# A planned decoder layer: buffers at the places that the plan gave them, from a first build that plans and a second that emits

## The chip, the cores and the metric

The kernel runs on one core of a Trainium2 chip. The metric is the device time of one execution in microseconds (us), as the median of several runs. One execution was also taken with the hardware profiler; its rows are what the prediction argues from.

## The reference

One hybrid decoder layer on 512 tokens of width 1024, all in float32:

```
h = rms_norm(x, mix_norm_g);  proj = h @ w_in           # 512 + 512 + 768 + 24 + 2048 columns
u, q, kv, nsa_g, merge_g = split(proj)
y_pool = pooling_mixer(u) @ w_pool_out                  # windows 2, 4, 8, 16; four 128-wide groups
y_nsa  = nsa_mixer(q, kv, sigmoid(nsa_g)) @ w_nsa_out   # 8 heads of 64, 2 kv groups, 3 branches:
                                                        #   compressed blocks, selected blocks, window
x = x + (gate_pool * y_pool + gate_nsa * y_nsa) @ w_out # gates: sigmoid of merge_g
h = rms_norm(x, ffn_norm_g)
gate_pre, val = split(h @ w_up)                         # 2 x 2816 columns
out = x + (silu(causal_dwconv(gate_pre)) * val) @ w_down
```

## The kernel before, in words

Activations lie transposed (features on the 128 partitions, 512 tokens along the row). Every float32 factor is split into a high part and a rest, both of a type that TensorE (PE) multiplies in one pass, so a product is three matmuls: high by high, high by rest, rest by high. A weight tile arrives in `wraw` by a transfer that SyncE (SP) issues; ScalarE (ACT) makes `whi`, and the rest `wlo` comes either from a subtraction on VectorE (DVE) or from an accumulating transfer that GpSimd (POOL) issues. In the attention part the q and k tiles (`qp`, `kp`) are normalised and rotated by DVE, transposed by PE against `ident` (in the constants `cs`) and copied and split into `qt` and `kt`. The second half of the layer, from the merge of the two mixers on, uses a seven-product scheme for most 2x2 blocks of weights (tiles `r1`, `r2`, `s3` and their parts `sh`, `sl`).

The stages lie in the profile about so: the first projections 0 to 60 us, attention with the remaining projections mixed in 60 to 260, the merge and output projection 260 to 345, the feed-forward part 345 to 640, the last down projection 640 to 675.

**What sets the order.** The layer is not emitted as it is written. The class `Plan` records every call as an `Op`, with dependences by tile region, and `emit` runs a small model of the engines (`run`, with costs from `price`) under many settings: which of two PE streams goes first, how late a transfer lands. A trial's order is run again, held fixed, under four settings of lateness and rate (`TRIALS`); the order with the smallest sum of modelled ends is emitted, call by call. All recorded calls are therefore issued from one line, and every row of the profile bears the line L431.

**What sets the places.** `Plan.tile` asks a pool for a tile under a tag with so many buffers: 60 pages `pg` of 128 x 512, rings of three for `wraw`, `whi` and `wlo`, ten `pp`, six `pt`, and in PSUM two banks `mm`, three `tr`, one `av` and `sc` with the rest. In the model, a new tile takes the place that came free first (`past = min(f)` in `run`, `free` keyed by tag). In the build, the framework's pool chooses among the places of the tag by itself. An instruction that first writes a tile waits for the users of the tile that had the place before.

Of the kernel before, what the change touches and what calls it, by code (L numbers as in the profile page):

```python
# [2 lines left out]

# [5 lines left out]
F32 = mybir.dt.float32  # L9
# [6 lines left out]
P = 128  # L16
T = 512
NT = 4
D = 1024
KD = 8  # L20
# [47 lines left out]
RATE = 331000.0  # L68
SHARE = 1.5
LANDS = (0.8, 0.8, 1.2, 1.2, 2.0, 2.0)  # L70
TRIALS = ((0.5, RATE), (0.8, RATE), (1.4, RATE), (0.8, 0.9 * RATE))
AHEAD = 4
RUN = 12

# [21 lines left out]
class Op:  # L96
# [3 lines left out]
    def __init__(self, i, eng, stream):  # L100
        self.i, self.eng, self.stream = i, eng, stream
        self.calls, self.cost, self.tail, self.land = [], 0.0, 0.0, 0
        self.deps, self.succ, self.allocs, self.tiles = set(), [], [], set()
        self.due, self.port = 0.0, False
# [9 lines left out]
        return call  # L114


class Plan:
    OUT = ("out", "accum_out", "ap")
    FIFO = ("wraw", "whi", "wlo")

    def __init__(self, nc):
# [81 lines left out]
    def price(self, eng, method, outs, ins, a, kw):  # L203
        n = max(_cols(x) for x in outs + ins)
        if method == "dma_start":
            x = outs[0]
            size = x.ap[0][1] * _cols(x) * 4 if hasattr(x, "ap") else 0
            return (0.87 if eng == "POOL" else 0.45), 0.0, size * (2.0 if kw.get("accum_op") is not None else 1.0)
        if eng == "PE":
            n = _cols(a[2])  # L210
            return max(n / 2250.0 + (0.005 if n < 300 else 0.0), 0.109), 0.17, 0
        if eng == "ACT":
            c = 0.19 + n * 0.000835
            if any(_cols(x) == 1 for x in ins):
                c += 0.09
            if kw.get("accum_out") is not None:
                c += 0.19
            if a[2] in (AF.Sin,):
                c += 1.28
            return c, 0.0, 0  # L220
        if eng == "DVE":
            wide = [x for x in ins if _cols(x) > 1]
            if method == "tensor_tensor_reduce":
                return 0.24 + n * 0.00105, 0.0, 0
            if len(wide) > 1 or method == "tensor_reduce" or any(x.tensor.name in self.psum for x in wide):
                return 0.15 + n * (0.00105 if method != "scalar_tensor_tensor" else 0.00114), 0.0, 0
# [5 lines left out]
    def run(self, key, reserve, land, rate=RATE, fixed=None):  # L232
        ops = self.ops
        ahead = 0 if fixed else AHEAD
        engs = ("PE", "ACT", "DVE", "POOL", "SP")
        free = {t: [(0.0, "")] * c for t, c in self.caps.items()}
# [19 lines left out]
        def finish(o):  # L256
            for n in o.tiles:
                left[n] -= 1
                if not left[n]:
                    free[self.tag[n]].append((max(u.fin for u in self.users[n]) + 0.06, n))  # L260
            for s in o.succ:
                s.left -= 1
                s.ready = max(s.ready, o.start + o.cost if s.eng == o.eng and not o.land else o.fin + 0.06)
                if not s.left and s.eng != "PE":
                    pool[s.eng].append(s)

        def settle(limit):
            while True:
                act = [(1.0 if e == "POOL" else SHARE, l) for e, l in queue.items() if l and l[0][0] <= now[0]]
                both = sum(q for q, _ in act)  # L270
                t = min((l[0][0] for l in queue.values() if l and l[0][0] > now[0]), default=1e18)
                head = None
                if act:
                    q, l = min(act, key=lambda x: x[1][0][1] / x[0])
                    if now[0] + l[0][1] / q * both <= t:
                        t, head = now[0] + l[0][1] / q * both, l
                if t > limit:
                    return False
                for q, l in act:
                    l[0][1] -= (t - now[0]) * q / both  # L280
                now[0] = t
                if head:
                    o = head.pop(0)[2]
                    o.fin = t + (self.lands[o.i] if land is None else land)
                    finish(o)
                    return True

        def when(o):
            t = o.ready
            for n in o.allocs:  # L290
                g = self.tag[n]
                f = free[g]
                if g in nxt and self.rank[n] != nxt[g] or n in self.early and self.early[n] != line[0]:
                    return None
                if len(f) <= (0 if g != "pg" else ahead if n in self.early else reserve if o.stream == "f" else 0):
                    return None
# [31 lines left out]
        while len(order) < len(ops):  # L328
            best = None
# [24 lines left out]
            for n in o.allocs:  # L354
                g = self.tag[n]
                f = free[g]
                past = min(f)
                f.remove(past)
                for u in self.users.get(past[1], ()):
# [8 lines left out]
        settle(1e17)  # L368
        while settle(1e17):
            pass  # L370
        return order, max(clock.values())

    def dues(self, order):
        lost, end, due = 0.0, 0.0, {}
# [11 lines left out]
    marks = ()  # L386

    def emit(self, tries, reserve):
        for n, u in self.users.items():
            for o in u:  # L390
                o.tiles.add(n)
        for o in self.ops:
            for d in o.deps:
                self.ops[d].succ.append(o)
        start = [float(o.i) for o in self.ops]
        part = [sum(m <= o.i for m in self.marks) for o in self.ops]
        parts = len(self.marks) + 1
# [2 lines left out]
        for cut in (0,) + CUTS:  # L400
            key, seen = start, []
            for i in range(tries + (MORE if cut else 0)):
# [4 lines left out]
                self.lands = [lands[p] for p in part]  # L407
                order, _ = self.run(key, reserve, None)
# [5 lines left out]
                for late, rate in TRIALS:  # L414
                    again, span = self.run(key, 0, late, rate, fixed)
                    spans += span
                    end = 0.0
                    for o in again:
                        if o.eng == "PE":
                            lost[part[o.i]] += max(0.0, o.start - end)  # L420
                            end = o.start + o.cost
                seen.append((lost, used, lands))
                if best is None or spans < best[0]:
                    best = (spans, order)
            last = seen[:tries]
            ahead = [c for c in CUTS if c > cut]
            if ahead:
                _, frozen, frozen_land = min(seen, key=lambda x: sum(x[0][:ahead[0]]))
        for o in best[1]:
            for method, a, kw in o.calls:  # L430
                getattr(self.real[o.eng], method)(*a, **kw)  # L431


@with_exitstack
def hybrid_layer(ctx: ExitStack, tc: tile.TileContext, xT, xa, pos, par, cst, poolw, w1, wa, wb, wf,
                 wpo, wno, wout, wup, wdn, wdz, out):
    nc = tc.nc
    pl = Plan(nc)
# [1193 lines left out]
```

## Time and profile before

| | before |
|---|---|
| median of 3 runs | 680.16 us (680.01 to 680.59) |
| the profiled execution's own time | 680.19 us |
| its span, first to last instruction | 678.1 us |
| PE busy (matmuls) | 673.4 us, 99% of the span |
| weight loads of PE (PEld) busy | 609.1 us, 90% |
| DVE busy | 545.2 us, 80% |
| ACT busy | 458.7 us, 68% |
| POOL busy | 109.0 us, 16% |
| mean rate of the transfers | 172 GB/s |

A matmul's row begins where it starts and ends where its last result is modelled to be written, so rows of neighbours overlap; how fast PE really works is read from the distance of starts, and a stretch without a row is an idle PE. "Idle before" names what ended a gap. SPq and POOLq rows are issues of transfers.

### The profile page before, as it was taken

How to read it: one execution, taken by the hardware profiler on the slowest of the kernel's cores; microseconds unless marked ns; L12 is line 12 of the kernel's file. 1: busy time of each engine (PE TensorE's matmuls, PEld its weight loads, DVE VectorE, ACT ScalarE, POOL GpSimd, SP SyncE). 2: the span in 40 equal slices, each digit the busy share in tenths (PEclk: the TensorE clock that was granted, in tenths of full speed). 3: DMA queues.
4: the chain of work that ended last, by engine and by line, in shares of the span. 5: the costliest groups of instructions: out<-in, count | busy, mean ns of one | idle time of the engine just before them, and what ended most of it. 6: DMA issues, size and time to landing. Idle time of an engine off the chain costs nothing.

```text
span 678.1 us, 11960 instructions
## 1 busy us (share of the span) xinstructions
PE 673.4 (99%) x4294; PEld 609.1 (90%) x4294; DVE 545.2 (80%) x1198; ACT 458.7 (68%) x857; POOL 109.0 (16%) x138
## 2 busy tenths in 40 slices
PE   9999999999999999999999999999999999999998
PEld 8898888888888888988889999999999999999997
DVE  6869678788887867788888998887778787899983
ACT  7666577776677765347788867677657677675741
POOL 0010111010110110001322312222213122220121
PEclk9999999999999999999999999999999999999999
DMA  8469646263565555846977958779858678553774
GB/s 306 145 156 264 172 108 187 67 171 99 143 167 134 143 134 181 312 146 203 232 166 176 194 144 203 194 170 208 190 160 190 168 161 211 134 115 129 191 181 109
DMA packets 51179, 116.41 MB, mean 172 GB/s; under 512 B 5808, under 2 KB 9264, under 8 KB 51120
## 3 DMA queue, kind: packets, MB, share of 16 engines
q1 hardware_dynamic: 32688, 76.44, 33.9%
q0 software_dynamic: 18288, 39.07, 32.6%
q8 instruction: 34, 0.56, 0.3%
q14 instruction: 25, 0.20, 0.1%
q10 hardware_dynamic: 144, 0.14, 0.1%
HBM read 70.28 MB, written 6.29 MB: 113 GB/s over the span
## 4 chain that ended last, share of the span: by engine, by line
PE 99%; DMA 1%; SPq 0%; ACT 0%; DVE 0%; issue 0%
PE mm L431 38%; PE tr L431 36%; PE sc L431 13%; PE av L431 12%; DMA wraw<-wa 1%; SPq L431 0%; ACT whi L431 0%; DVE o L431 0%
## 5 line engine op out<-in xcount | busy, mean ns | idle before, releaser
L431 ACT ACTIVATE whi<-wraw 128x1024 fp32r<-128x1024 f32 (+4 forms) x99 | 91.9, 930 | 40.9 <-PE sc L431 14.7
L431 DVE TENSOR_TENSOR wlo<-wraw,whi 128x1024 fp32r<-128x1024 f32 (+3 forms) x73 | 74.0, 1015 | 5.1 <-ACT whi L431 4.3
L431 PE MATMUL tr<-tl,sh 128*128 128x256 f32 x261 | 73.1, 280 | 0.0
L431 PE MATMUL mm<-xh,whi 128*128 128x512 f32 x176 | 70.7, 402 | 0.0
L431 PE MATMUL tr<-th,sh 128*128 128x256 f32 x250 | 70.4, 282 | 0.0
L431 PE MATMUL tr<-th,sl 128*128 128x256 f32 x250 | 70.4, 282 | 0.0
L431 PE MATMUL mm<-xh,wlo 128*128 128x512 f32 x176 | 68.9, 391 | 0.0
L431 PE MATMUL mm<-xl,whi 128*128 128x512 f32 x176 | 68.6, 390 | 0.0
L431 POOL DMA_DIRECT2D sl<-r x46 | 39.8, 866 | 149.8 <-ACT sl L431 104.8
L431 POOL DMA_DIRECT2D wlo<-wraw x26 | 22.3, 858 | 231.7 <-ACT wlo L431 178.8
L431 PEld LDWEIGHTS tr<-tl,sh 128*128 128x128 f32 x261 | 49.3, 189 | 0.2
L431 PEld LDWEIGHTS tr<-th,sh 128*128 128x128 f32 x250 | 47.0, 188 | 0.7
L431 PEld LDWEIGHTS tr<-th,sl 128*128 128x128 f32 x250 | 47.0, 188 | 0.0
L431 ACT ACTIVATE wlo<-wraw 128x1024 fp32r<-128x1024 f32 x26 | 27.6, 1060 | 19.3 <-PE mm L431 18.4
L431 PEld LDWEIGHTS mm<-xh,wlo 128*128 128x128 f32 x176 | 33.0, 188 | 7.3
L431 PEld LDWEIGHTS mm<-xl,whi 128*128 128x128 f32 x176 | 33.1, 188 | 6.2
L431 ACT ACTIVATE pp<-pp,asm 128x384 f32<-128x384 f32 (+3 forms) x64 | 35.4, 556 | 4.9 <-DVE asm L431 4.9
L431 PEld LDWEIGHTS mm<-xh,whi 128*128 128x128 f32 x176 | 33.1, 188 | 6.1
L431 DVE SCALAR_TENSOR_TENSOR ft<-fg,pr,ft 128x511 f32<-128x511 f32 (+1 forms) x44 | 32.9, 749 | 7.0 <-ACT ft L431 6.3
L431 POOL DMA_DIRECT2D sl<-wraw x26 | 22.4, 862 | 84.7 <-ACT sl L431 68.5
L431 ACT ACTIVATE sh<-wraw 128x512 fp32r<-128x512 f32 x52 | 32.3, 620 | 4.1 <-DVE wraw L431 4.0
L431 ACT ACTIVATE sl<-r 128x512 fp32r<-128x512 f32 x46 | 28.6, 622 | 9.3 <-DMA r<-wup 5.4
(443 smaller groups left out, 2134.4 us busy)
## 6 DMA issues: line engine op xcount, KB each, us to landing
wlo<-wraw POOLq DMA_DIRECT2D x26, 512.0 KB, 4.6
wraw<-wup SPq DMA_DIRECT2D x23, 512.0 KB, 4.1
sl<-r POOLq DMA_DIRECT2D x46, 256.0 KB, 4.8
wraw<-wf SPq DMA_DIRECT2D x22, 512.0 KB, 3.6
r<-wup SPq DMA_DIRECT2D x42, 256.0 KB, 5.7
sl<-wraw POOLq DMA_DIRECT2D x26, 256.0 KB, 4.2
wraw<-wdn SPq DMA_DIRECT2D x16, 320.0 KB, 3.7
sl<-s POOLq DMA_DIRECT2D x17, 256.0 KB, 5.0
```

Source lines behind the costliest of these rows:

```text
L431: getattr(self.real[o.eng], method)(*a, **kw)
```

## The change

Four things are altered, all in the planning code.

The kernel function is built twice. In the first build, `Plan` has no `made`; it plans, and instead of emitting it raises `Planned` with two lists, the order of the ops and for each tile the number of the place that the model gave it. The second build is given these lists: `tile` makes each place a pool entry of its own (tag and place number, one buffer), and `emit` writes the ops in the stored order.

In the model, `free` now holds for each place when it comes free, its number and its last tile; `run` notes in `taken` which place each tile took, and a run with a fixed order can also hold the places fixed (`slots`), so that a tile waits for its own place rather than for the first free one.

The trials by which an order is judged grow from four to seven: three with a lateness drawn at random for each op (0.5 to 1.8, for one op in 25 up to 3.0 more).

The price of a PE matmul changes: a float32 matmul that is not a transpose counts as two passes, and 0.005 is added below 500 columns rather than below 300.

```
+class Planned(Exception):
+    pass
...
     def tile(self, pool, shape, dt, name, tag, bufs, psum=False):
-        t = pool.tile(list(shape), dt, name=name, tag=tag, bufs=bufs)
+        if self.made:
+            slot = self.made[1][len(self.homes)]
+            t = pool.tile(list(shape), dt, name=name, tag="%s.%d" % (tag, slot), bufs=1)
+        else:
+            t = pool.tile(list(shape), dt, name=name, tag=tag, bufs=bufs)
         n = t.tensor.name
+        self.homes.append(n)
...
-            return max(n / 2250.0 + (0.005 if n < 300 else 0.0), 0.109), 0.17, 0
+            passes = 2 if method == "matmul" and a[1].dtype == F32 else 1
+            return passes * max(n / 2250.0 + (0.005 if n < 500 else 0.0), 0.109), 0.17, 0
...
-                t = max(t, min(f)[0])
+                if slots is None:
+                    t = max(t, min(f)[0])
+                else:
+                    at_slot = [x[0] for x in f if x[1] == slots[n]]
+                    if not at_slot:
+                        return None
+                    t = max(t, at_slot[0])
...
     def emit(self, tries, reserve):
+        if self.made:
+            for i in self.made[0]:
+                for method, a, kw in self.ops[i].calls:
+                    getattr(self.real[self.ops[i].eng], method)(*a, **kw)
+            return
...
+        trials = [([late] * len(self.ops), rate) for late, rate in TRIALS]
+        for seed in range(RANDOM):
+            r = random.Random(seed)
+            trials.append(([r.uniform(0.5, 1.8) + (r.random() < 0.04) * r.uniform(0.0, 3.0) for _ in every], RATE))
...
-        for o in best[1]:
-            for method, a, kw in o.calls:
-                getattr(self.real[o.eng], method)(*a, **kw)
+        raise Planned(best[1], [best[2].get(n, 0) for n in self.homes])
```

Both programs hold the same instructions, each with the same operands; what differs is their order on an engine, the places, and so the waits. POOL's order is the same row for row. PE's order is the same up to the transposes of q and k near 53 us and again from the end of attention on; between them blocks of 2 to 12 matmuls change places. ACT, DVE and SP differ in many places by a few rows. Three places follow; the change's rows bear L413, the line from which its second build issues.

**SP, the first loads.** `wraw` are weights of the first projection (`wa`), `xr` and `x0` parts of x. Before:

```order
L431 DMA wraw_82<-wa 128x512
L431 DMA x0_67<-xa 128x256
L431 DMA wraw_82<-wa 128x256
L431 DMA xr_87<-xT 128x512
L431 DMA wraw_91<-wa 128x768
L431 DMA xr_88<-xT 128x512
L431 DMA wraw_97<-wa 128x768
L431 DMA xr_94<-xT 128x512
```

Now:

```order
L413 DMA wraw_82<-wa 128x512
L413 DMA x0_67<-xa 128x256
L413 DMA wraw_82<-wa 128x256
L413 DMA wraw_91<-wa 128x768
L413 DMA xr_87<-xT 128x512
L413 DMA wraw_97<-wa 128x768
L413 DMA xr_88<-xT 128x512
L413 DMA xr_94<-xT 128x512
```

The weights of the second round (`wraw_91`) are issued ahead of x's second part (`xr_87`), and those of the third (`wraw_97`) ahead of `xr_88`.

**PE, the transposes of the first two k tiles**, `tr_193`, among the matmuls of the first gate projection, `mm_231`, near 59 us. Before:

```order
L431 MATMUL mm_231<-xh_113,whi_229 128x512
L431 MATMUL mm_231<-xl_114,whi_229 128x512
L431 MATMUL mm_231<-xh_113,wlo_230 128x512
L431 MATMUL mm_231<-xh_119,whi_229 128x512
L431 MATMUL mm_231<-xl_120,whi_229 128x512
L431 MATMUL mm_231<-xh_119,wlo_230 128x512
L431 MATMUL mm_231<-xh_133,whi_229 128x512
L431 MATMUL mm_231<-xl_134,whi_229 128x512
L431 MATMUL mm_231<-xh_133,wlo_230 128x512
L431 MATMUL tr_193<-cs_65,kp_151 128x128 x2
L431 MATMUL tr_193<-cs_65,kp_152 128x128 x2
L431 MATMUL tr_199<-cs_65,qp_149 128x128 x4
```

Now:

```order
L413 MATMUL tr_193<-cs_65,kp_151 128x128 x2
L413 MATMUL tr_193<-cs_65,kp_152 128x128 x2
L413 MATMUL mm_231<-xh_113,whi_229 128x512
L413 MATMUL mm_231<-xl_114,whi_229 128x512
L413 MATMUL mm_231<-xh_113,wlo_230 128x512
L413 MATMUL mm_231<-xh_119,whi_229 128x512
L413 MATMUL mm_231<-xl_120,whi_229 128x512
L413 MATMUL mm_231<-xh_119,wlo_230 128x512
L413 MATMUL mm_231<-xh_133,whi_229 128x512
L413 MATMUL mm_231<-xl_134,whi_229 128x512
L413 MATMUL mm_231<-xh_133,wlo_230 128x512
L413 MATMUL mm_236<-xh_85,whi_234 128x512
```

The four k transposes stand nine matmuls earlier, and the transposes of the third q tile (`tr_199`) no longer follow them.

**DVE, the rotation of those tiles** (`kp_151`, `kp_152` of k, `qp_149` of q; `rt` are products with the sine), near 54 to 58 us. Before:

```order
L431 SCALAR_TENSOR_TENSOR vv_182<-mm_181,rstd_70,vv_182 128x4x64
L431 TENSOR_TENSOR qp_149<-tr_77,small_81 128x512
L431 TENSOR_TENSOR qt_188<-tr_186,qt_188 64x512
L431 TENSOR_TENSOR kp_151<-kp_151,gkv_140 128x256
L431 TENSOR_TENSOR kp_152<-kp_152,gkv_140 128x256
L431 TENSOR_TENSOR rt_184<-kp_151,rope_138 128x64
L431 TENSOR_TENSOR rt_185<-kp_152,rope_138 128x64
L431 TENSOR_TENSOR rt_189<-qp_149,ropeq_143 128x128
L431 TENSOR_TENSOR kp_151<-kp_151,rope_138 128x4x16
L431 TENSOR_TENSOR kp_152<-kp_152,rope_138 128x4x16
L431 TENSOR_TENSOR qt_187<-tr_186,qt_187 64x512
L431 TENSOR_TENSOR kp_151<-kp_151,rt_184 128x4x16
```

Now:

```order
L413 TENSOR_TENSOR kp_151<-kp_151,gkv_140 128x256
L413 TENSOR_TENSOR kp_152<-kp_152,gkv_140 128x256
L413 TENSOR_TENSOR rt_184<-kp_151,rope_138 128x64
L413 TENSOR_TENSOR rt_185<-kp_152,rope_138 128x64
L413 TENSOR_TENSOR qp_149<-tr_77,small_81 128x512
L413 TENSOR_TENSOR kp_151<-kp_151,rope_138 128x4x16
L413 TENSOR_TENSOR kp_152<-kp_152,rope_138 128x4x16
L413 TENSOR_TENSOR kp_151<-kp_151,rt_184 128x4x16
L413 TENSOR_TENSOR kp_152<-kp_152,rt_185 128x4x16
L413 SCALAR_TENSOR_TENSOR vv_182<-mm_181,rstd_70,vv_182 128x4x64
L413 TENSOR_TENSOR qt_188<-tr_186,qt_188 64x512
L413 TENSOR_TENSOR rt_189<-qp_149,ropeq_143 128x128
```

The k tiles' last additions move ahead of `vv_182`, of the two splits of the first q tile (`qt_188`, `qt_187`, the latter now the next row) and of `rt_189`.

**ACT in a feed-forward step** near 387 us: `u1` and `tr` are copies out of and between PSUM banks, `whi_1036` the high part of a down projection's weights, `ft_985` the gate's silu, `sh` and `sl` parts of weight sums. Before:

```order
L431 ACTIVATE u1_982<-tr_980 128x256
L431 ACTIVATE whi_1036<-wraw_1035 128x640
L431 ACTIVATE ft_985<-ft_985 128x512
L431 ACTIVATE tr_1005<-mm_1004 128x256
L431 ACTIVATE sl_1019<-r2_1015 128x512
```

Now:

```order
L413 ACTIVATE u1_982<-tr_980 128x256
L413 ACTIVATE sh_1003<-wraw_988 128x512
L413 ACTIVATE tr_1005<-mm_1004 128x256
L413 ACTIVATE whi_1036<-wraw_1035 128x640
L413 ACTIVATE ft_985<-ft_985 128x512
```

The copy `tr_1005`, which the next products of PE accumulate onto, now stands ahead of `whi_1036` and `ft_985`.

More of the change, by code (lines that the diff above doesn't have):

```diff
@@ L1 @@
 import math
+import random
 from contextlib import ExitStack, contextmanager, nullcontext
@@ L71 @@
 TRIALS = ((0.5, RATE), (0.8, RATE), (1.4, RATE), (0.8, 0.9 * RATE))
+RANDOM = 3
 AHEAD = 4
@@ L119, with __init__ @@
     FIFO = ("wraw", "whi", "wlo")
-    def __init__(self, nc):
+    def __init__(self, nc, made):
+        self.made, self.homes = made, []
         self.real = {"PE": nc.tensor, "ACT": nc.scalar, "DVE": nc.vector, "POOL": nc.gpsimd, "SP": nc.sync}
@@ L230, in price, with run @@
         return 0.33 + n * 0.0025, 0.0, 0
-    def run(self, key, reserve, land, rate=RATE, fixed=None):
+    def run(self, key, reserve, lands, rate=RATE, fixed=None, slots=None):
         ops = self.ops
@@ L235, in run @@
         engs = ("PE", "ACT", "DVE", "POOL", "SP")
-        free = {t: [(0.0, "")] * c for t, c in self.caps.items()}
+        free = {t: [(0.0, i, "") for i in range(c)] for t, c in self.caps.items()}
+        taken = {}
         nxt = {t: 0 for t in self.FIFO}
@@ L259, in finish @@
                 if not left[n]:
-                    free[self.tag[n]].append((max(u.fin for u in self.users[n]) + 0.06, n))
+                    free[self.tag[n]].append((max(u.fin for u in self.users[n]) + 0.06, taken[n], n))
             for s in o.succ:
@@ L283, in settle @@
                     o = head.pop(0)[2]
-                    o.fin = t + (self.lands[o.i] if land is None else land)
+                    o.fin = t + lands[o.i]
                     finish(o)
@@ L356, in run @@
                 f = free[g]
-                past = min(f)
+                past = min(f) if slots is None else [x for x in f if x[1] == slots[n]][0]
                 f.remove(past)
-                for u in self.users.get(past[1], ()):
+                taken[n] = past[1]
+                for u in self.users.get(past[2], ()):
                     u.hand.append(o)
@@ L370, in run @@
             pass
-        return order, max(clock.values())
+        return order, max(clock.values()), taken
     def dues(self, order):
@@ L394, in emit @@
                 self.ops[d].succ.append(o)
+        every = range(len(self.ops))
+        trials = [([late] * len(self.ops), rate) for late, rate in TRIALS]
+        for seed in range(RANDOM):
+            r = random.Random(seed)
+            trials.append(([r.uniform(0.5, 1.8) + (r.random() < 0.04) * r.uniform(0.0, 3.0) for _ in every], RATE))
         start = [float(o.i) for o in self.ops]
@@ L406, in emit @@
                 lands = [frozen_land[p] if p < cut else LANDS[i % len(LANDS)] for p in range(parts)]
-                self.lands = [lands[p] for p in part]
-                order, _ = self.run(key, reserve, None)
+                order, _, slots = self.run(key, reserve, [lands[p] for p in part])
                 used = key
@@ L413, in emit @@
                 spans, lost = 0.0, [0.0] * parts
-                for late, rate in TRIALS:
-                    again, span = self.run(key, 0, late, rate, fixed)
+                for late, rate in trials:
+                    again, span, _ = self.run(key, 0, late, rate, fixed, slots)
                     spans += span
@@ L423, in emit @@
                 if best is None or spans < best[0]:
-                    best = (spans, order)
+                    best = (spans, [o.i for o in order], slots)
             last = seen[:tries]
@@ L428, in emit @@
                 _, frozen, frozen_land = min(seen, key=lambda x: sum(x[0][:ahead[0]]))
-        for o in best[1]:
-            for method, a, kw in o.calls:
-                getattr(self.real[o.eng], method)(*a, **kw)
+        raise Planned(best[1], [best[2].get(n, 0) for n in self.homes])
 @with_exitstack
 def hybrid_layer(ctx: ExitStack, tc: tile.TileContext, xT, xa, pos, par, cst, poolw, w1, wa, wb, wf,
-                 wpo, wno, wout, wup, wdn, wdz, out):
+                 wpo, wno, wout, wup, wdn, wdz, out, made=None):
     nc = tc.nc
-    pl = Plan(nc)
+    pl = Plan(nc, made)
     PE, ACT, DVE, POOL, SP = pl.engines
@@ L1622 @@
     arrays = _layout(**inputs)
-    nc = _bacc.Bacc("TRN2", target_bir_lowering=False, num_devices=1, dynamic_dma_scratch_size=4096)
-    args = [nc.dram_tensor(n, a.shape, _mybir.dt.from_np(a.dtype), kind="ExternalInput").ap()
-            for n, a in arrays.items()]
-    args.append(nc.dram_tensor("out", (KD, P, T), F32, kind="ExternalOutput").ap())
-    with _tile.TileContext(nc) as tc:
-        hybrid_layer(tc, *args)
+    made = None
+    for _ in range(2):
+        nc = _bacc.Bacc("TRN2", target_bir_lowering=False, num_devices=1, dynamic_dma_scratch_size=4096)
+        args = [nc.dram_tensor(n, a.shape, _mybir.dt.from_np(a.dtype), kind="ExternalInput").ap()
+                for n, a in arrays.items()]
+        args.append(nc.dram_tensor("out", (KD, P, T), F32, kind="ExternalOutput").ap())
+        try:
+            with _tile.TileContext(nc) as tc:
+                hybrid_layer(tc, *args, made=made)
+        except Planned as plan:
+            made = plan.args
     r = _run(nc, [arrays], core_ids=[0])
```

## The prediction

> **What bounds the kernel now.** I read the page's busy times first, then PE's waits, then the stretches, then the chain that ended last.
>
> ```profile
> span 678.1 us, 11960 instructions
> PE 673.4 (99%) x4294; PEld 609.1 (90%) x4294; DVE 545.2 (80%) x1198; ACT 458.7 (68%) x857; POOL 109.0 (16%) x138
> ...
> PE mm L431 <- POOL ones L431: 1.0, 1, 1.0
> PE sc L431 <- ACT whi L431: 0.3, 1, 0.3
> ```
>
> The two last rows are the whole list of PE's waits: 1.0 us before its very first matmul and 0.3 us once more, in 678.1 us. The next rows are stretches (us, then busy time of each engine with its number of instructions, then granted clock) and, last, their sum over six stretches from 6.45 to 674.76.
>
> ```profile
> 60.00:260.00 200.00, 200.00 (x1069) 169.00 (x1068) 157.79 (x477) 144.90 (x305) 21.25 (x29) 1.00 0.56 144
> 345.00:400.00 55.00, 55.00 (x445) 54.07 (x444) 50.01 (x93) 44.10 (x83) 12.18 (x15) 1.00 0.77 174
> sum 668.31, PE 668.31 PEld 604.59 DVE 543.25 ACT 455.93 POOL 108.55; mean PE 111.39 PEld 100.76 DVE 90.54 ACT 75.99 POOL 18.09
> ```
>
> From 6.45 us to 674.76 us, PE is busy for 668.31 of 668.31 us. Since a matmul's row lasts longer than the distance to the next start, a wait of some tenths could hide in that. So I look at distances, in the chain of waits (start, us, what) and in the group of one kind of matmul.
>
> ```profile
> 131.80 2.79 PE mm L431 x12
> 207.58 2.72 PE mm L431 x12
> 358.42 2.83 PE tr L431 x24
> 378.28 2.83 PE tr L431 x24
> 656.30 2.84 PE tr L431 x24
> ...
> L431 PE MATMUL mm<-xh,whi 128*128 128x512 f32 x176 | 70.7, 402 | 0.0
> ```
>
> Twelve 512-wide matmuls take 2.72 to 2.79 us, or 0.227 to 0.233 each; 24 of width 256 take 2.83 or 2.84, or 0.118 each, early in the feed-forward part and at its end alike. The stream is evenly packed: no stage has slower matmuls that better placement could speed up. The kernel is bound by the number of its matmuls, with a head before 6.45 and a tail behind 674.76:
>
> ```profile
> 1.64 4.31 DMA wraw<-wa
> 6.45 0.74 PE sc L431 x4
> ...
> 674.48 0.28 PE L431 MATMUL tr<-yth,sl 128*128 128x256 f32 x1
> 674.80 0.42 DVE L431 TENSOR_TENSOR o<-x,tr 128x256 f32<-128x256 f32 x1 [1.00 <-PE tr L431]
> ```
>
> The head is the first weights' landing at 5.95 (1.64 + 4.31) and a cast; the tail is one addition and a store, 678.1 - 674.76 = 3.3 us.
>
> **The change part by part.** The trials, the new price of a matmul and the two builds run on the host while the program is made; none is an instruction, so each costs nothing on the chip except through the order and the places they lead to. No matmul is added, removed or resized. PE's 668.31 us therefore stay, and the sum asks only what the new order and places add as waits.
>
> *What can be gained.* Of the waits, the 1.0 us ends with the constant that POOL writes and stays. The 0.3 us ends with the cast of the weights that land at 5.95; that transfer is SP's third issue before and now, so it stays too. Bound: 0 to 0.3 us.
>
> *SP's first loads.* The landings are read from what waited for them:
>
> ```profile
> 6.80 0.72 ACT L431 ACTIVATE xh<-xr,x 128x512 fp32r<-128x512 f32 x1 [0.40 <-DMA xr<-xT]
> 7.95 0.83 ACT L431 ACTIVATE whi<-wraw 128x768 fp32r<-128x768 f32 x1
> 9.83 0.87 PE L431 MATMUL tr<-whi,xh 128*128 128x512 f32 x3
> ```
>
> The part of x lands by 6.80 and the weights of round two by 7.95, so 1.15 us lie between them (an upper estimate, since ACT may have come later than the landing). Swapped, the weights land by about 5.95 + 1.15 = 7.10 and their cast ends at 7.93; x lands by 7.95 and its cast ends at 8.67. PE needs both at 9.83. Before, the later of the two ended at 7.95 + 0.83 = 8.78. The margin goes from 1.05 to about 1.16 us: cost nothing; PE's first round covers it, and without that cover a late cast would stand in full.
>
> *The k transposes near 59 us.* All rows of this step, DVE first:
>
> ```profile
> 53.72 0.47 DVE L431 SCALAR_TENSOR_TENSOR vv<-mm,rstd,vv 128x256 fp32r<-128x256 f32 x1
> 55.02 0.69 DVE L431 TENSOR_TENSOR qt<-tr,qt 64x512 fp32r<-64x512 f32 x1 [0.23 <-ACT qt L431]
> 56.70 0.28 DVE L431 TENSOR_TENSOR rt<-qp,ropeq 128x128 f32<-128x128 f32 x1
> 57.28 0.69 DVE L431 TENSOR_TENSOR qt<-tr,qt 64x512 fp32r<-64x512 f32 x1
> 58.00 0.36 DVE L431 TENSOR_TENSOR kp<-kp,rt 128x64 f32<-128x64 f32 x2
> 61.80 0.69 DVE L431 TENSOR_TENSOR kt<-tr,kt 64x512 fp32r<-64x512 f32 x1 [0.89 <-ACT kt L431]
> 62.52 0.69 DVE L431 TENSOR_TENSOR th<-mm,rb 128x512 f32<-128x512 f32 x1
> 63.77 0.29 DVE L431 TENSOR_TENSOR qp<-qp,rt 128x128 f32<-128x128 f32 x1
> ...
> 59.49 1.06 ACT L431 ACTIVATE wlo<-wraw 128x1024 fp32r<-128x1024 f32 x1 [3.41 <-PE mm L431]
> 59.29 0.60 PE L431 MATMUL tr<-cs,kp 128*128 128x128 f32 x4
> 64.25 0.60 PE L431 MATMUL tr<-cs,qp 128*128 128x128 f32 x4
> ```
>
> PE comes to the k transposes nine matmuls earlier: 9 x 0.228 = 2.05 us, at 57.24 instead of 59.29. On DVE the last additions move ahead of four instructions: 0.47 + 0.69 + 0.28 + 0.69 = 2.13 us. They ended at 58.36 and should end at 56.23. The first transposes had 59.29 - 58.2 (the first of the two additions) = about 1.1 us of margin and keep it: 2.13 gained against 2.05 spent. The next narrow place is the fourth q tile: its addition ends at 64.06 and PE starts at 64.25, a margin of 0.19. There PE comes three matmuls earlier, 0.68 us, and DVE's `th` of 0.69 moves behind the addition: the margin stays at 0.20. It even grows where ACT no longer puts its 1.06 us `wlo` ahead of the copy for which DVE stood 0.89 us. If that cover failed, each tenth late there would be a tenth of PE's time. I take nothing; bounds -0.1 and +0.9 us (DVE standing for ACT again, at the new place).
>
> *ACT in the feed-forward.*
>
> ```profile
> 387.10 0.73 ACT L431 ACTIVATE whi<-wraw 128x640 fp32r<-128x640 f32 x1
> 388.25 0.38 ACT L431 ACTIVATE tr<-mm 128x256 f32<-128x256 f32 x1
> 399.55 3.43 PE sc L431 x15
> ```
>
> The copy still cannot run before PE has its sum, at 388.25, so ACT now stands for it, and the weight cast behind it starts near 388.6 instead of 387.10: 1.5 us late. DVE's rest of those weights is late by as much, and so is SP's next load into that ring. The down projection that uses them starts at 399.55, 11 us after the cast. ACT is busy 44.10 of 55 us in this stretch, so it makes good the 1.5 us. Cost nothing; the cover is the distance of 11 us.
>
> *The places.* The trace shows no address and no cost of one. Bounds come from the twelves, which lie on different tiles: the 176 first matmuls of the quoted kind stand for 176 x 3 / 12 = 44 twelves; had all the shortest or the longest time instead of the middle, they would give 44 x 0.035 = 1.5 us either way. I take 0, since no stretch differs. As waits, places matter where a new tile must wait for the old one's users; PE's list shows no such wait before, so nothing is there to remove, and one that the plan adds counts as an order's delay.
>
> The sum: 678.1 + 0 + 0 + 0 = 678.1 of span; the profiled execution took 680.19, 2.1 more, and lies within 0.03 of the median 680.16. Forecast: **680.2 us**.
>
> **The rivals.** (a) *Slower: the supply at the start of the feed-forward.* In 345 to 400 us DVE is busy 50.01 of 55, and weight parts arrive just before use:
>
> ```profile
> L431 POOL DMA_DIRECT2D sl<-r x3: 860/862/862, 374.5 to 383.8; - x3
> DMA to landing us min/median/max: 3.4/7.1/7.8
> 382.60 0.28 PE L431 MATMUL tr<-th,sl 128*128 128x256 f32 x1
> ```
>
> A part issued at 374.5 that takes 7.8 us lands at 382.3, and PE reads such a part at 382.60: 0.3 us of margin. A feature repeats every (378.28 - 358.42) / 2 = 9.93 us, so this stretch holds five. If the swaps make these parts late by one DVE instruction of 0.69, PE waits 0.4 in each: 5 x 0.4 = 2.0 us, 682.2 us. It decides from the fourth feature on. For it: the thin margin, and ACT and DVE rows that trade places. Against it: PE's and POOL's orders are unchanged there, and the work ahead of these very parts on ACT is the same.
>
> (b) *Faster: hidden waits go.* The 44 twelves fall to 2.72 us each: 1.5 us less, 678.7. For it: the spread. Against it: a twelve's end is a neighbour's start, so the spread comes with the neighbour's kind.
>
> (c) *Faster: free time behind the weight loads.* Between 60 and 260 us, where most of PE's order changes, no weights are loaded for 200.00 - 169.00 = 31.0 us. If the new order filled a tenth of that, 3.1 us, the time would be 677.1. The Trainium skill, "Perfetto Trace Analysis", section "Identifying the Most-Contended Engine", says that matmul busy time is a poor measure of how near PE is to its limit, and that the busy share of weight loads is a good one. By that rule the 90% leave room. The trace speaks against it: with 0.228 us from start to start and a load per matmul, loads pause because 512 columns stream, not because something is late.
>
> (d) *The change does not do what it says:* the second build's places differ from the plan, or come to the same waits. Then the time is that of the order alone, 680.2 as well.
>
> **How the numbers follow.** The forecast has a chance of 0.74, (d) 0.03, (a) 0.17, (b) 0.04, (c) 0.02. A measurement of this kernel can tell about 0.2%, 1.36 us, from no change. So "same", 678.8 to 681.5, has 0.74 + 0.03 = 0.77; slower 0.17; faster 0.04 + 0.02 = 0.06. The forecast's own range is 679.6 (0.3 gained, and 0.3 for the runs) to 681.1 (the 0.9 at the k transposes). Widened above to (a) with 0.2 for the runs, and below by some more tenths towards (b), it is 679.3 to 682.4, which leaves out (b), (c) and a longer (a), about 0.1.
>
> **What would show it.** If right, the changed kernel's page has PE at 99%, waits of PE of about 1.3 us in all, again 2.72 to 2.79 for a twelve and 2.83 for 24, and `sc` near 6.45 us. The k transposes start near 57.2 us with DVE's `kp` done near 56.2, and DVE's 0.89 us before `kt` is gone. ACT shows a gap before `tr<-mm` near 388 with `whi` behind it. (a) would show as waits of PE for POOL or as stretched distances between 345 and 400 us, and `sc` at 399.55 later by as much. What would make me wrong: any wait of PE over 1.4 us in sum, above all in attention, where its order changed in blocks that I did not price one by one, or a span whose distances differ with the places.

## The result, and the profile after

The changed kernel takes 683.42 us in the median of 6 runs (682.84 to 684.20), the kernel before 680.20 us beside it: 1.0051 times as long, 95% interval [1.0041, 1.0062]. That is 3.2 us more, 2.8 to 4.2 by the interval. The forecast was 680.2, its range 679.3 to 682.4. The profiled execution was the slowest of the six, 684.20 us, with a span of 682.2; its clock row shows 9 in every slice, as before.

First the page's busy times after, and the list of PE's waits:

```profile
span 682.2 us, 11940 instructions
...
PE 677.2 (99%) x4294; PEld 610.2 (89%) x4294; DVE 546.2 (80%) x1198; ACT 459.2 (67%) x857; POOL 109.0 (16%) x138
```

```profile
PE mm L413 <- POOL ones L413: 1.0, 1, 1.0
PE tr L413 <- DMA sl<-r: 0.7, 1, 0.7
```

PE is as busy as before by its share, with the same 4,294 matmuls, and its busy time grew by 677.2 - 673.4 = 3.8 us. The list has 1.7 us of waits against 1.3. So the lost time is hardly to be found under waits: the same matmuls take longer. The stretches show where. Of the kernel before, two rows (those of 60 to 260 and of 345 to 400 us stand in the prediction), and then four of the kernel after (us, busy time of PE, weight loads, DVE, ACT and POOL, each with its number of instructions, then the granted clock):

```profile
260.00:345.00 85.00, 85.00 (x420) 72.06 (x419) 68.92 (x115) 50.12 (x81) 11.30 (x16) 1.00 0.72 218
...
400.00:640.00 240.00, 240.00 (x1723) 226.53 (x1722) 199.50 (x346) 166.38 (x294) 54.20 (x63) 1.00 0.72 170
```

```profile
60.00:260.00 200.00, 200.00 (x1069) 168.78 (x1068) 159.18 (x478) 144.00 (x302) 21.31 (x29) 1.00 0.58 147
260.00:345.00 85.00, 85.00 (x413) 70.95 (x412) 68.09 (x109) 47.82 (x78) 9.57 (x14) 1.00 0.70 215
345.00:400.00 55.00, 54.29 (x433) 52.95 (x433) 48.78 (x95) 44.97 (x83) 13.79 (x16) 1.00 0.79 178
400.00:640.00 240.00, 240.00 (x1709) 225.52 (x1708) 199.28 (x344) 164.79 (x292) 53.44 (x62) 1.00 0.71 168
```

At the same clock of 1.00 and with PE busy throughout, 413 matmuls fit between 260 and 345 us where 420 did, and 1,709 between 400 and 640 where 1,723 did. Attention, 60 to 260, shows no difference by this count. The chain that ended last gives the distance from one matmul to the next, since a group's time there runs from its first start to the start of the group behind it. Before, and after:

```profile
304.99 10.88 PE tr L431 x48
...
399.55 3.43 PE sc L431 x15
```

```profile
305.74 11.09 PE tr L413 x48
...
376.25 8.91 DMA sl<-r
...
402.28 3.46 PE sc L413 x15
```

The 48 matmuls of the merge, 512 columns each, took 10.88 / 48 = 226.7 ns from start to start, and now 11.09 / 48 = 231.0. Nothing else is between them in either kernel: no wait, no other kind of matmul. The transfer of 8.91 us in the last fence is the part that PE waited 0.7 us for, near 384 us.

### The profile page after: what moved, and what is told of

It reads as the page before. It is cut to its first block, busy times and chain, and to the rows that moved or that the text cites. A ratio compares the mean times of both kernels' runs of the same rounds, so it can differ in the third digit from the quotient of the medians.

```text
span 682.2 us, 11940 instructions
## 1 busy us (share of the span) xinstructions
PE 677.2 (99%) x4294; PEld 610.2 (89%) x4294; DVE 546.2 (80%) x1198; ACT 459.2 (67%) x857; POOL 109.0 (16%) x138
## 4 chain that ended last, share of the span: by engine, by line
PE 96%; DMA 2%; issue 1%; ACT 0%; POOL 0%; SPq 0%; DVE 0%; POOLq 0%
PE mm L413 38%; PE tr L413 34%; PE sc L413 13%; PE av L413 11%; DMA sl<-r 1%; DMA r<-wup 1%; ACT L413 0%; POOL sl L413 0%; SPq L413 0%; ACT sl L413 0%; DVE o L413 0%; ACT u L413 0%; ACT ft L413 0%; POOL ones L413 0%; POOLq L413 0%
## 5 line engine op out<-in xcount | busy, mean ns | idle before, releaser
L413 ACT ACTIVATE whi<-wraw 128x1024 fp32r<-128x1024 f32 (+4 forms) x99 | 91.9, 930 | 46.5 <-PE sc L413 20.0
L413 DVE TENSOR_TENSOR wlo<-wraw,whi 128x1024 fp32r<-128x1024 f32 (+3 forms) x73 | 74.0, 1015 | 5.5 <-ACT whi L413 3.6
L413 PE MATMUL tr<-tl,sh 128*128 128x256 f32 x261 | 73.4, 281 | 0.0
L413 PE MATMUL tr<-th,sl 128*128 128x256 f32 x250 | 70.5, 282 | 0.7 <-DMA sl<-r 0.7
L413 PE MATMUL mm<-xh,whi 128*128 128x512 f32 x176 | 70.7, 402 | 0.0
L413 PE MATMUL tr<-th,sh 128*128 128x256 f32 x250 | 70.5, 282 | 0.0
L413 PE MATMUL mm<-xh,wlo 128*128 128x512 f32 x176 | 68.9, 392 | 0.0
L413 PE MATMUL mm<-xl,whi 128*128 128x512 f32 x176 | 68.7, 390 | 0.0
L413 POOL DMA_DIRECT2D sl<-r x46 | 39.7, 864 | 153.8 <-ACT sl L413 112.9
L413 POOL DMA_DIRECT2D wlo<-wraw x26 | 22.4, 860 | 231.9 <-ACT wlo L413 175.2
L413 PEld LDWEIGHTS tr<-tl,sh 128*128 128x128 f32 x261 | 49.2, 188 | 0.2
L413 PEld LDWEIGHTS tr<-th,sl 128*128 128x128 f32 x250 | 47.2, 189 | 0.9 <-DMA sl<-r 0.9
L413 PEld LDWEIGHTS tr<-th,sh 128*128 128x128 f32 x250 | 47.1, 188 | 0.8
L413 ACT ACTIVATE wlo<-wraw 128x1024 fp32r<-128x1024 f32 x26 | 27.5, 1058 | 18.6 <-PE mm L413 16.9
L413 PEld LDWEIGHTS mm<-xh,wlo 128*128 128x128 f32 x176 | 33.0, 188 | 7.4
L413 ACT ACTIVATE pp<-pp,asm 128x128 f32<-128x128 f32 (+3 forms) x64 | 35.4, 556 | 6.0 <-DVE asm L413 5.7
L413 PEld LDWEIGHTS mm<-xl,whi 128*128 128x128 f32 x176 | 33.1, 188 | 6.2
L413 PEld LDWEIGHTS mm<-xh,whi 128*128 128x128 f32 x176 | 33.1, 188 | 6.1
L413 DVE SCALAR_TENSOR_TENSOR ft<-fg,pr,ft 128x511 f32<-128x511 f32 (+1 forms) x44 | 32.9, 747 | 5.7 <-ACT ft L413 5.3
L413 ACT ACTIVATE sh<-wraw 128x512 fp32r<-128x512 f32 x52 | 32.3, 621 | 5.4 <-DVE wraw L413 5.0
L413 POOL DMA_DIRECT2D sl<-wraw x26 | 22.4, 862 | 83.5 <-ACT sl L413 74.4
L413 PE MATMUL sc<-yl,whi 128*128 128x512 f32 x88 | 34.6, 394 | 0.0
```

The lines of the kernel that those rows point to most:

```text
L413: getattr(self.real[self.ops[i].eng], method)(*a, **kw)
```

## The experiments

Three theories. **A**: the addresses of the places set the distance between matmuls. **B**: the new order costs the time. **C**: the weight rings cost it, because they now stand among the other places. The program's allocation table gives the addresses. In the kernel before, all pages lie in one piece, as do the rings. In the changed kernel each place lies where it was first used, with small tiles of 128 to 768 bytes in between. Where an expectation calls a place large, it means a multiple of 2,048 bytes: 60 pages, 9 ring places, 16 places of the two smaller pools, five single stores.

### The two halves of the change, and the new order on aligned places

The changed kernel with its order, reuse and waits, but with the large places created first:

```diff
+            if self.made and not self.places:          # second build, before the first tile in SBUF
+                for key, size in self.made[2]:
+                    pool.tile([128, size // 4], F32, name="at", tag="%s.%d" % key, bufs=1)
...
+        keys.sort(key=lambda k: size[k] % 2048 > 0)    # made[2]: places in order of first use, large first
```

> The changed kernel with its own order, its own reuse of places and the same waits; only the addresses differ: every place whose size is a multiple of 2048 bytes stands ahead of all small ones, so that all of them begin at 128 bytes past a multiple of 2048. (In the changed kernel small tiles stand between them, and the places begin at 128, 256, 640, 768, 1408, 1536, 1728, 1792 or 1952 past one; in the kernel before 60 of them begin at 128.) Theory A, the start addresses set the distance from one matmul to the next: between 260 and 345 us, where the 512-wide distance rose from about 227 ns to 231, it falls back to 227, and with it the 1.2 us that this stretch lost; of the 1.5 us that crept in after 400 us some 1 to 1.5 go. The wait of 0.7 to 0.9 us near 384 stays. 683.4 - 2.2 to 2.7 = 680.7 to 681.2 us. Theory B, the order costs the time: 683.4. Theory C, weight rings standing among the other places cost it, since they are still there: 683.4, with 231 ns.

Measured: 679.54 us (11 runs), 0.9996 of the kernel before, [0.9987, 1.0005]. The whole loss is gone, with the order of the changed kernel. Its chain of waits:

```profile
304.17 10.88 PE tr L418 x48
...
398.91 3.41 PE sc L418 x15
...
529.18 3.40 PE sc L418 x15
...
655.42 2.84 PE tr L418 x24
```

The distance is 226.7 ns again, and the groups of 15 in the feed-forward part take 3.40 us, less than the 3.43 of the kernel before. The rings still stand among the pages, so C falls; the order is the changed one, so B falls for the most part. More came back than A expected (it said 680.7 to 681.2): attention and the feed-forward part had lost more than I had read from the first comparison, and PE has no wait near 384 here.

Now the order alone: `tile` asks for the pool's tags in both builds.

```diff
-        if self.made:
-            slot = self.made[1][len(self.homes)]
-            t = pool.tile(list(shape), dt, name=name, tag="%s.%d" % (tag, slot), bufs=1)
-        else:
-            t = pool.tile(list(shape), dt, name=name, tag=tag, bufs=bufs)
+        t = pool.tile(list(shape), dt, name=name, tag=tag, bufs=bufs)
```

> The changed kernel's order, emitted by the second build, but each buffer asks for its pool entry as before, and the framework chooses the places: the order alone. Theory A (addresses): the places stand as before, 60 of them alike modulo 2048, so distances of 227 ns between 260 and 345 us, and the time is that of the kernel before plus the wait near 384, if that is the order's own: 680.2 to 681.1 us. Theory B (the order): 683.4. Theory C: like A.

Measured: 680.74 us (11 runs), 1.0017, [1.0005, 1.0029]. Its 48 matmuls of the merge take 10.88 us again, but its list of PE's waits has one of its own:

```profile
PE tr L409 <- ACT u L409: 1.2, 1, 1.2
```

ACT was late with `u` because it stood for a weight transfer; that transfer's issue on SP is the next fence, and ACT's rows the one behind it:

```profile
392.28 0.33 SPq L409 DMA_DIRECT2D wraw<-wup  x1
```

```profile
396.83 1.06 ACT L409 ACTIVATE whi<-wraw 128x1024 fp32r<-128x1024 f32 x1 [2.36 <-DMA wraw<-wup]
397.80 0.61 ACT L409 ACTIVATE ft<-ft 128x512 f32<-128x512 f32 x1
398.31 0.37 ACT L409 ACTIVATE u<-tr 128x256 f32<-128x256 f32 x1
```

With the planned places of the first experiment and the same order, the load is issued 2.8 us earlier, and ACT does not stand for it:

```profile
389.48 0.33 SPq L418 DMA_DIRECT2D wraw<-wup  x1
```

```profile
394.57 1.06 ACT L418 ACTIVATE whi<-wraw 128x1024 fp32r<-128x1024 f32 x1 [0.47 <-PE mm L418]
```

So in the traced execution the planned places, as a rule of reuse, spared this order a wait of 1.2 us. Both kernels have the same rows on every engine and 226.7 ns in the merge, and their medians on one chip, 679.54 and 680.74, differ by 1.2 us too; but not all of that is the wait. Behind it the groups of 15 take 3.43 us here against 3.41 and 3.40 above:

```profile
400.42 3.43 PE sc L409 x15
...
657.37 2.84 PE tr L409 x24
```

The lag behind the first experiment is 1.5 us at the first of these rows and 1.95 at the second, so some 0.4 us come from slower matmuls. How often the wait comes is not known from one trace. That the place of the ring is what SP waited for is my reading of these rows; no run took that one wait apart.

The places alone: the old price and the four old trials, which give the old order on every engine.

```diff
-            passes = 2 if method == "matmul" and a[1].dtype == F32 else 1
-            return passes * max(n / 2250.0 + (0.005 if n < 500 else 0.0), 0.109), 0.17, 0
+            return max(n / 2250.0 + (0.005 if n < 300 else 0.0), 0.109), 0.17, 0
...
-RANDOM = 3
+RANDOM = 0
```

> The other half: the old price and the four old trials, which give the order of the kernel before on every engine, with each buffer put at its planned place, a pool entry of its own created at first use, as in the changed kernel: the places alone. Theory A (addresses): between 260 and 345 us distances of 231 ns and about 1.2 us lost, about 1.5 us more behind 400; without the wait near 384, 680.2 + 2.7 = 682.9 us, or 0.9 more if that wait too is the places' doing. Theory B (the order): 680.2. Theory C: like A.

Measured: 681.85 us (7 runs), 1.0031, [1.0020, 1.0042]. From its chain of waits:

```profile
305.02 11.01 PE tr L412 x48
```

The distance is 229.4 ns, so A's effect comes without the new order, though smaller than in the changed kernel. The table of addresses has the same remainders in both, so I take it that the other order puts other tiles on the misaligned places; no run shows that. The places alone cost 2.0 us, the order alone 0.9, both together 3.2.

The old order with planned, aligned places joins the two diffs:

> The order of the kernel before with planned places, laid out so that every place of a multiple of 2048 bytes begins at 128 past one, the 16 pages of the two smaller pools and the three large stores too, which in the kernel before begin at 640, 1408, 1536, 1920 and 1952. Theory A (addresses): 680.2 or less; if the 512-wide matmuls of attention and of the projections, 228.6 to 229.3 ns on average between 60 and 260 us and 231.6 before 60, fell to 227, it would be 620 x 2.0 + 116 x 4.6 ns = 1.8 us less, 678.4; where they come from the short matmuls in between, nothing, 680.2. Theory B (the order): 680.2. Theory C (rings among the places): 682.9, as in the experiment with the places alone.

Measured: 679.52 us (11 runs), 0.9993, [0.9984, 1.0002]. From its chain of waits:

```profile
304.67 10.88 PE tr L417 x48
...
399.29 3.40 PE sc L417 x15
```

And its stretch from 60 to 260 us:

```profile
60.00:260.00 200.00, 200.00 (x1070) 169.01 (x1069) 157.92 (x478) 144.88 (x305) 21.29 (x29) 1.00 0.56 144
```

The feed-forward groups of 15 fall from 3.43 to 3.40 us, but attention hardly changed (1,070 matmuls against 1,069). The 1.8 us that I had hoped for there are not in the addresses. So neither order on aligned places is measurably faster than the kernel before, and each gains 0.3 to 0.4 us on it, within the noise, where the changed kernel lost 3.2.

### The changed kernel once more

> The changed kernel once more, unchanged, to see whether the wait near 384 us and the distances repeat. If distances come from the addresses, 231.1 ns again between 290 and 343 us. If the wait of 0.7 to 0.9 us at 384 comes from the order and places, it is there again and the time is 683.4; if it came from one slow transfer (8.9 us there instead of 6.3 in the kernel with equal addresses), it is absent and the profiled execution is at about 682.5.

Measured: 683.22 us (5 runs), 1.0050, [1.0036, 1.0064], and the profiled execution has no wait near 384 us. Its list of waits:

```profile
PE mm L413 <- POOL ones L413: 1.0, 1, 1.0
PE sc L413 <- ACT whi L413: 0.2, 1, 0.2
```

The distances repeat, and matmul by matmul: by the starts in the two traces, 317 distances between matmuls of 512 columns, 260 to 345 us, vary from 224 to 238 ns, and each is the same in both executions to 1 ns. Chance meetings with transfers or other engines would hardly repeat like that. Its chain of waits, to be read beside that of the first experiment, whose order is the same:

```profile
305.34 11.09 PE tr L413 x48
...
400.91 3.46 PE sc L413 x15
...
531.99 3.47 PE sc L413 x15
...
659.05 2.85 PE tr L413 x24
```

The same matmuls start 1.17, 2.00, 2.81 and 3.63 us later: a lag that grows without a step, 3.6 of the 3.7 us between the medians. So the loss is there without the wait near 384. The wait is no accident of one execution either: of the ten profiles with this order and planned places, six have it, 0.4 to 0.8 us each (the first one and, further down, the rings moved by 256 and by 128 bytes, the odd pages by 128 and by 64, and all places by 128); neither of the two profiles with the old order and planned places does. In five of the six the transfer took 8.6 to 9.1 us, in one 7.4; where there is no wait, it took 6.3 to 8.3. These are the transfers of that one part, first of the changed kernel's first profile, then of the first experiment (bytes, us to landing):

```profile
sl<-r POOLq DMA_DIRECT2D x1, 256.0 KB, 8.9
```

```profile
sl<-r POOLq DMA_DIRECT2D x1, 256.0 KB, 6.3
```

### Which addresses

The large places of the changed kernel begin at 128, 256, 640, 768 and more bytes past a multiple of 2,048. The next runs start from the first experiment (all alike) and move some places behind one small tile, so that they begin a given step further. The rule of `keys.sort` is all that changes; for odd pages and a step of 256:

```diff
+        def place(k):
+            if size[k] % 2048:
+                return 1 if k[0] == "t_gq" else 3      # a tile of 256 bytes; the other small ones last
+            return 2 if k[0] == "pg" and k[1] % 2 else 0
+        keys.sort(key=place)
```

The tile is `ones` for 512, `vg` for 128 and two of `asm` for 64. For the rings the last condition is `k[0] in self.FIFO`, for all places `True`.

> The changed kernel with all large places aligned alike (the first experiment), except that the 30 pages with an odd number stand behind one 256-byte tile, so that they begin 256 bytes further (384 past a multiple of 2048 instead of 128). Consecutive matmuls then read pages of both kinds. If a step of 256 bytes between consecutive reads disturbs the stream: distances of 229 to 232 ns between 290 and 343 us and a time 2 to 3 us above the 679.5 of the first experiment. If only the number of different remainders or the small tiles in between matter: 226.7 ns and 679.5.

Measured: 678.95 us in one run, beside 679.86 for the kernel before. The row of its chain of waits that answers to those above (so in each run that follows):

```profile
304.04 10.88 PE tr L418 x48
```

> The same with a step of 512 bytes between odd and even pages. If equality modulo 2048 is what counts, 229 to 232 ns and 2 to 3 us more, as with 256. If equality modulo 512 is enough (the kernel before has some tiles at 640 past a multiple of 2048, and its distances beside them stayed at 226.5), 226.7 ns and 679.5 us.

Measured: 680.24 us in one run.

```profile
304.85 10.88 PE tr L418 x48
```

> The same with all pages alike, and only the nine places of the weight rings 256 bytes further. In the merge and the output projection the moving operand is a page and the weights come from the rings. If what counts is where one moving operand begins against the next, 226.7 ns between 290 and 343 us and 679.5; if it is the weights against the moving operand, 229 to 232 ns and 2 to 3 us more.

Measured: 680.49 us in one run, with one wait of 0.5 us near 384.

```profile
304.79 10.88 PE tr L418 x48
```

Steps of 256 and 512 bytes leave the distance at 226.7 ns. So the remainder modulo 2,048, on which the first expectations were built, is not what counts, and neither is it that a small tile stands between. Modulo 256, the table of addresses reads: before, 88 of the 90 large places at 128; after, 64 at 128 and 24 at 0. That led to the next four.

> The changed kernel with all large places aligned alike, except that the 30 odd pages stand behind one 128-byte tile and begin at 256 past a multiple of 2048 instead of 128. Steps of 256 and of 512 bytes changed nothing (226.67 ns between 290 and 343 us); in the changed kernel the places begin at 128 and 640 (both 128 past a multiple of 256) and at 256, 768 and 1792 (all multiples of 256). If the remainder modulo 256 counts, this one tile of 128 bytes brings the distances back to 229 to 232 ns and the time to 682.5 to 683.5 us. If not (if it needs many remainders, or the small tiles themselves), 226.67 ns and 679.5.

Measured: 684.23 us (5 runs), 1.0061, [1.0047, 1.0075].

```profile
306.74 11.05 PE tr L418 x48
```

One tile of 128 bytes ahead of half the pages brings the whole loss back, 230.2 ns and 4.2 us. (The profiled execution, the slowest of the five with 685.72 us, has two waits besides, 0.8 us for that transfer and 0.5 for a cast of weights.)

> The same 128-byte tile stands ahead of all 90 large places instead of half the pages: all begin at 256 past a multiple of 2048, all alike. If it is the change from one read to the next that costs, 226.67 ns and 679.5 us. If places at a multiple of 256 are slow as such, 229 to 232 ns everywhere and 682 us or more.

Measured: 680.46 us in one run, beside 680.01, with waits of 0.3 and 0.6 us, at 378 and 383. Its chain:

```profile
304.09 10.88 PE tr L418 x48
```

All places at a multiple of 256 give 226.7 ns as well. Neither remainder is slow by itself; a mixture is.

> All pages at 128, and only the nine places of the weight rings at 256 past a multiple of 2048. Between 290 and 343 us moving operands come from pages and weights from rings. If only the moving operands have to agree with each other, 226.67 ns there and about 679.5 us, with some loss where rings are the moving operand, before 60 us; if weights against moving operand count, 229 to 232 ns and 682 us or more.

Measured: 686.80 us in one run, beside 680.01.

```profile
307.07 11.16 PE tr L418 x48
```

Here every page is alike and only the weight rings begin elsewhere: 232.5 ns, the worst of all, and 6.8 us more than the kernel before, with a wait of 0.4 us for that transfer among them. So it is not enough that the moving operands (what PE streams past the loaded weights) agree with each other; what PE loads as weights must agree with what it streams. The rings also hold `wraw`, which ACT, DVE and transfers use and PE never reads; no run moved `whi` and `wlo` without it.

> As with 128 bytes, but the odd pages begin only 64 bytes further (192 past a multiple of 2048). If the remainder modulo 128 or less does not matter, 226.67 ns and 679.5; if any difference modulo 256 does, 229 to 232 ns and 2 to 4 us more than 679.5.

Measured: 686.14 us in one run.

```profile
307.55 11.11 PE tr L418 x48
```

A step of 64 bytes costs no less than one of 128: 231.5 ns, with one wait of 0.5 us for that transfer.

## Why the prediction was wrong

**The step that failed is the term for the places.** I took 0 and bounded it by 1.5 us either way. It measured 3.6 us: the lag between two kernels with the same order, reuse and waits that differ in addresses alone. Against the kernel before, the whole change cost 3.2. Two choices went wrong.

The value. "I take 0, since no stretch differs" rested on three groups of 24 at 2.83 and 2.84. Those are matmuls of 256 columns, which hardly react to the places: the last such group shown above takes 2.84 us with aligned places and 2.85 in the changed kernel. Nor do the twelves of attention tell what places can do. In the first experiment, with all large places alike, they still spread:

```profile
85.17 2.95 PE mm L418 x12
...
174.51 2.72 PE mm L418 x12
...
254.43 2.77 PE mm L418 x12
```

So putting their spread down to the neighbours was right, or at least not against the runs; taking that spread for what places can cost was the mistake. (The range of 2.72 to 2.79 also left out two twelves of 2.94 and 2.95 near 82 and 86 us, which stay so in the changed kernel.) That the kernel before showed no cost of a place fits its table of addresses, where 88 of 90 large places agree modulo 256. The merge would have been the place to look: the 48 matmuls there stood at 226.7 ns before, the low end of the twelves too (2.72 / 12), and 48 in a row have no neighbours of another kind. A stream that stands at the low end can hardly gain by other places, but it can lose. The bounds should have been near 0 and a loss, not 1.5 either way.

The bound. It counted 44 twelves, the 528 matmuls of one kind. The first group of these hardly changed:

```profile
L413 PE MATMUL mm<-xh,whi 128*128 128x512 f32 x176 | 70.7, 402 | 0.0
```

It has the same 70.7 us as before. There are 1,464 matmuls of 512 columns in the program by the groups of the kernel before, and the places touch all of them. The spread that I had in hand, 0.227 to 0.233, would have given 1,464 x 0.006 = 8.8 us; the worst layout tried took 686.80 - 680.01 = 6.8 us more than the kernel before. That the two lie near each other is luck, since the spread was not the places' doing. From the trace before alone no bound could be had; a run with one small tile among the pages would have given it.

**The rivals.** (a) named the right matmul: near 384 us PE did wait for `sl<-r`, 0.7 us, in the first profile. But the price of 5 x 0.4 was wrong. The wait came in one feature and not in five, and it is absent from the second profile of the same kernel, which lost as much. Its 682.2 lies near the result by accident. (b) looked at the right quantity, the distances, but put them down to hidden waits and had the wrong sign. No rival had the places make the distances grow. (c) falls: the time went up, and the weight loads between 60 and 260 us were busy for 168.78 us against 169.00, so that free time was not filled. The Trainium skill, "Perfetto Trace Analysis", "Identifying the Most-Contended Engine", takes the share of PE's weight loads as a measure of the headroom. That share was 90% before and 89% in a kernel 3.2 us slower, so it did not show this loss. (d) falls too: the order alone took 680.74, and the planned places change the addresses and, in one trace, a wait of 1.2 us.

**What held.** The number of matmuls, at the same granted clock. The first loads: nothing lost; the wait of 0.3 us that I said would stay is gone in the first profile and 0.2 in the second, within the bound. The k transposes, for which the rows after are PE's, DVE's (two views, one kernel):

```profile
57.24 0.60 PE L413 MATMUL tr<-cs,kp 128*128 128x128 f32 x4
```

```profile
55.43 0.36 DVE L413 TENSOR_TENSOR kp<-kp,rt 128x64 f32<-128x64 f32 x2
...
59.70 0.69 DVE L413 TENSOR_TENSOR kt<-tr,kt 64x512 fp32r<-64x512 f32 x1 [1.13 <-ACT kt L413]
```

PE starts them at 57.24. That this is the forecast to the hundredth is luck, since the second profile of the same kernel has them at 56.80; the nine matmuls are not. DVE's additions end at 55.79 instead of 56.23, and its stand before `kt` did not vanish but grew from 0.89 to 1.13 us, off the path: PE waits for nothing there. ACT in the feed-forward part also went as said, the copy first, behind a short stand, and the cast after it:

```profile
390.95 0.37 ACT L413 ACTIVATE tr<-mm 128x256 f32<-128x256 f32 x1 [0.52 <-PE mm L413]
391.23 0.73 ACT L413 ACTIVATE whi<-wraw 128x640 fp32r<-128x640 f32 x1
```

It costs nothing with the planned places (the first experiment). With the framework's places the same order lost 1.2 us some 10 us later, in the one trace of it, through a load into a weight ring, the ring that I named as late next. So "cost nothing" holds for the changed kernel, and the cover is thinner than the 11 us that I gave it.

"A span whose distances differ with the places" stood among the things that would make me wrong, and it did. So did waits of PE over 1.4 us in sum: the first profile has 1.7, the second 1.2.

## What to carry to other kernels

When a change moves buffers, compare the distance between matmuls in the chain of waits (a group's time divided by its count) before looking for waits: PE showed 99% busy in both kernels. Create large buffers first and small ones last, or pad the small ones, so that everything PE streams and loads begins at the same remainder modulo 256 bytes (steps of 64 and 128 were slow here, smaller ones were not tried). And judge a planner's places on such a layout: here its order and its places were as good as the old ones, and only the addresses that came with them lost time.

## What the runs showed of the hardware that I had not expected

The time of a matmul of 512 columns, 128 rows, 4-byte data depends on where its operands begin in a partition. With all places alike modulo 256 bytes it is 226.7 ns from start to start (at 128 past and at 0 past); with half the pages 128 or 64 bytes off, 230.2 and 231.5; with the weights 128 bytes off from all pages, 232.5, or 2.6% more. Steps of 256 bytes (half the pages, or the weights) and of 512 (half the pages) leave it at 226.7. Matmuls of 256 columns hardly react: 24 of them took 2.84 us with aligned places and 2.85 in the changed kernel.

The Trainium skill, "SBUF — State Buffer", section "A bandwidth-pool intuition that's wrong (but worth ruling out)", gives PE a second, independent read port for loading weights. By that alone, where weights begin against the moving operand should not matter. The run with only the rings moved by 128 bytes says that it does, 226.7 ns against 232.5 and 6.8 us of 680, and the measurement decides.

Three things stay open. Whether moving operands that disagree only with each other cost anything: in the runs with odd pages moved they also disagree with the weights. Whether there is a price per disagreeing matmul at all: in the merge and output projection of the run with odd pages 128 bytes off, by the starts in its trace and the addresses in its table, 87 matmuls of 512 columns agree in remainder with their own and their neighbours' weights and pages. They take 231.3 ns to the next start in the mean, the other 227 take 230.2, so the cost does not stay with the matmul whose operand is off. And what in the chip does it: no run here looks behind the distances.
